# One layer of a streaming trunk: where the residual is added in the FFN down product

## The chip, the cores and the metric

The kernel runs on one core of a Trainium2 chip. The metric is the device time of one execution in microseconds (us). Before the change it is 1692.53 us, the median of three runs (1690.29 to 1696.99).

## The reference, cut to what matters

Everything is float32, 1024 tokens of width 1024. The change lies in the last product of the layer, the FFN down product, whose K is 3072 long, and in how its result is added to the residual stream `x`.

```python
D_MODEL, SEQ, D_FF = 1024, 1024, 3 * 1024
...
x = x + mix @ w_out[l]
h = rms_norm(x, norm2_w[l])
up = h @ ffn_w_up[l]
gate, val = jnp.split(up, [D_FF], axis=-1)
gate = causal_depthwise_conv(gate, ffn_conv_w[l], ffn_conv_b[l])
x = x + (jax.nn.gelu(gate) * val) @ ffn_w_down[l]
...
return rms_norm(x, norm_f_w)
```

## The kernel before, in words

All products run on TensorE (PE) in tiles of 128 x 512. To keep float32 precision, each operand is split into two parts (`split`, L167 and L168: ScalarE (ACT) casts the tile to a rounded part, VectorE (DVE) subtracts to get the rest), and three matmuls are done in place of one (`PASSES`).

Work is cut into jobs. A job has four results of 128 x 512, named (m, c), or (m, h) in a plain job. A plain job (`mm_std`, matmuls on L317) makes them with 96 matmuls. A fast job (`mm_fast`, matmuls on L347) uses seven products of 12 matmuls in place of eight (84 matmuls), on sums of blocks of both operands: on the weight side S1 to S4 (L235 to L251), on the other side T1 to T4 (`tsets`, L484 to L492). Its PSUM banks X, Y and Z are collected in two steps: `keep` copies a bank to SBUF on ACT (L362) while the bank goes on accumulating, and `total` adds a second bank on DVE (L371). Result (1, 0) alone comes out of bank X directly. A fast job is started before the one ahead of it has ended.

The FFN down product is the last stage. Its K of 3072 is cut into three groups g of 1024, and for each g there are four jobs t, of which t = 0 is plain and t = 1 to 3 are fast. Here the activations, written to DRAM (`ff_d`, L1006, by DMAs that GpSimd (POOL) issues) are the stationary blocks, loaded by L197 into `w` places, and the down weights `w_dn` are the moving operand, loaded by L1016 into `u` places and split there, or summed and split. The running sum over g is held in DRAM, in `x1_d`, which starts as the residual. For g < 2 each of the four results of a job is made so: a tile of `x1_d` is loaded (`pre_down`, L1052), DVE adds it (L365 in `keep` for three of the four results of a fast job, L1062 in `emit_down` for the other result and for all four of a plain job), and the sum is stored to `x1_d` (L1066). With g = 2 the sum stays in SBUF and goes into the final norm.

All loads and stores in this stage but those of L1006 are issued by SyncE (SP), which works through one list in order; an instruction that must wait holds up those behind it. The 78 `u` places are handed out oldest first, and a place that is handed out again is written only once its last user is done, which may be a DMA that still reads it. `build` makes the operand of the next group as long as at least 20 places are free. The order on each engine is set when the program is built, by a scheduler that goes by priority; `hp` raises it.

```python
def split(src, get=get):
    hi, lo = get(F32R), get(F32R)
    S.copy(hi, src)
    V.tensor_sub(lo, src, hi.bitcast(F32))
    return hi, lo
```

Of the kernel before, what the change touches and what calls it, by code (L numbers as in the profile page):

```python
# [15 lines left out]
ALU = mybir.AluOpType  # L16
# [68 lines left out]


class Units:
    """places of one shape in a pool, handed out oldest first in program order"""

    def __init__(self, pool, name, n, shape):  # L90
        self.pool, self.name, self.shape = pool, name, shape
# [7 lines left out]
    def get(self, dt=F32):  # L99
        i = self.q.popleft()  # L100
        self.count += 1
        t = self.pool.tile(self.shape, dt, tag=f"{self.name}{i}", name=f"{self.name}{i}_{self.count}")
        self.at[id(t)] = (i, t)
        return t

    def put(self, *tiles):
        for t in tiles:
            self.q.append(self.at.pop(id(t))[0])
# [20 lines left out]
def tile_trunk_layer(ctx, tc, x, positions, params, consts, normf, w_in, w_ro, w_lo,  # L129
                     w_out, w_up, w_dn, w_gate, out):  # L130
    nc = tc.nc
    V, S, G, PE, SY = nc.vector, nc.scalar, nc.gpsimd, nc.tensor, nc.sync
    ST = G if GQ else SY

    pool = ctx.enter_context(tc.tile_pool(name="sb", bufs=1))
# [8 lines left out]
    get, put = U.get, U.put  # L144
# [16 lines left out]
    def hp():  # L161
        return tc.high_priority(offset=1500)

    def split(src, get=get):
        """the two float32r parts of a float32 operand"""
        hi, lo = get(F32R), get(F32R)
        S.copy(hi, src)  # L167
        V.tensor_sub(lo, src, hi.bitcast(F32))  # L168
        return hi, lo
# [1 line left out]
    def drop(s):  # L171
        put(*s)

# [1 line left out]
    ORD_T = ("A11", "A12", "A21", "A22")  # L175

    class Job:
# [94 lines left out]
    back = deque()  # L272

    def build(budget, reserve=RESERVE):
        """go on with the operands that come next while there is room for them"""
        with hp():
            while builders and budget > 0 and len(U) >= reserve:
                c = next(builders[0], None)
                if c is None:
                    builders.popleft()  # L280
                else:
                    budget -= c
# [136 lines left out]
    def pair_src(w, i):  # L419
        return lambda m, kh: w[i, 2 * m + kh]  # L420

# [1 line left out]
    st = pool.tile([P, 16], F32, tag="st", name="st")  # L423
    nst = pool.tile([P, 5, 8], F32, tag="nst", name="nst")

    def rstd_of(dst, var, tmp):
        S.activation(tmp, var, AF.Sqrt)
        V.reciprocal(dst, tmp)
        V.tensor_mul(tmp, dst, dst)
        V.tensor_mul(tmp, tmp, var)  # L430
        V.tensor_scalar(tmp, tmp, -0.5, 1.5, ALU.mult, ALU.add)
        V.tensor_mul(dst, dst, tmp)

    def rms_scale(tiles, n, o=0):
        """1 / rms of n token tiles, one column each"""
        for t in range(n):
            for c in range(2):
                j = psa.get()
                if c == 0:
                    S.activation(j, tiles[t, c], AF.Square, accum_out=nst[:, c, o + t:o + t + 1])  # L440
                else:
                    V.scalar_tensor_tensor(j, tiles[t, c], 1.0, tiles[t, c], ALU.mult, ALU.mult,
                                           accum_out=nst[:, c, o + t:o + t + 1])
                psa.put(j)
        a, b, v, r, w = (nst[:, i, o:o + n] for i in range(5))
        V.tensor_add(v, a, b)
        V.tensor_scalar(v, v, 1.0 / D, EPS, ALU.mult, ALU.add)
        rstd_of(r, v, w)
        return r
# [56 lines left out]

    h1, keep = {}, {}

# [1 line left out]
    lt = pool.tile([P, 2, 8], F32, tag="lt", name="lt")  # L510
    lneg, lhalf = lt[:, 0, :], lt[:, 1, :]

# [17 lines left out]
        V.tensor_scalar(lhalf, s3, 4.0, None, ALU.mult)  # L530
        V.tensor_scalar(lneg, s3, -8.0, None, ALU.mult)

# [1 line left out]
    rot = {}  # L534

    def rotary_tables():
# [62 lines left out]
            rot["c", hf], rot["s", hf] = c, s  # L599
        put(pi_t, ang, m, a, f, r)  # L600

# [1 line left out]
    xl = {}  # L603
    tails = pool.tile([P, 2, 4], F32, tag="tails", name="tails")

# [96 lines left out]
        for w in wg:  # L702
            drop(w)

# [1 line left out]
    qk, vv, gg = {}, {}, {}  # L706
    rst = [pool.tile([P, 256], F32, tag=f"state{i}", name=f"state{i}") for i in range(2)]
    bst = pool.tile([P, 4, 6], F32, tag="bst", name="bst")
# [102 lines left out]
        if hd == HEADS - 1:  # L811
            put(*rot.values())

# [1 line left out]
    def emit_gate(which, n):  # L815
        def emit(m, h, src, unit):
            t = get() if unit is None else unit
# [3 lines left out]
        return emit  # L821

    def operand(op, fetch, sums=True):
        """the sets of an operand: first those of the plain product, then the sums"""
        for n in ("B11", "B21", "B12", "B22"):
            for j in range(4):
                t = fetch(n, j)
                op[n, j] = split(t)
                put(t)
                yield 0.6  # L830
        if sums:
            yield from tsets(op, fetch)
# [51 lines left out]
    gates = [(w, n) for n in range(4) for w in range(2)]  # L884
# [5 lines left out]
    for what in SEQ.split():  # L890
        if what == "g":
            add_gate()
        elif what[0] == "y":
            n = int(what[1])
            add(2 * n + 1, emit_y(n))
        elif what[0] == "x":
            n = int(what[1])
# [8 lines left out]
    def og_start(post=jobs[-2].post):  # L906
        builders.append(operand(og, from_dram(og_d), False))
        return post() if post else None
# [35 lines left out]
            mix[k, h] = split(mixf[k, h])  # L944
            put(mixf[k, h])

# [1 line left out]
    h2, keep2 = {}, {}  # L948
    for c in range(2):
        wo = {}  # L950
# [6 lines left out]
        for half in range(2):  # L957
            tl = {}
            for t in range(4):
# [4 lines left out]
                n = 0  # L964
# [22 lines left out]
            for w in wo.values():  # L987
                drop(w)

# [1 line left out]
    gv = {}  # L991

    def post_ff(i):
# [44 lines left out]
    run([Job(pair_src(w_up, i), h2, emit_to(gv), up_post(i), fast=i >= STD_U, last=i == NF - 1,  # L1038
             drop12=i == STD_U - 1) for i in range(NF)])

# [1 line left out]
    nf = []  # L1042
    fin = {}

    def x1_at(t, m, c):
        r0 = 512 * m + 128 * t
        return x1_d[r0:r0 + 128, TH * c:TH * c + TH]

    def pre_down(t):
        def pre(m, c):  # L1050
            acc = get()
            SY.dma_start(acc, x1_at(t, m, c))  # L1052
            return acc
        return pre

    def emit_down(g, t, fast):
        def emit(m, c, src, unit):
            if fast and unit is not None:
                acc = unit
            else:  # L1060
                acc = pre_down(t)(m, c)
                V.tensor_add(acc, src, acc)  # L1062
                if unit is not None:
                    put(unit)
            if g < 2:
                ST.dma_start(x1_at(t, m, c), acc)  # L1066
                put(acc)
                return
            fin[m, c] = acc
            square(m, c)  # L1070
            if (m, 1 - c) in fin:
                final(t, m)
        return emit

    def square(m, c):
        """what a finished tile adds to its rows' sum of squares; then the norm's weights"""
        j = psa.get()
        S.activation(j, fin[m, c], AF.Square, accum_out=nst[:, c, 2 + m:3 + m])
        psa.put(j)
        V.tensor_mul(fin[m, c], fin[m, c], nf[c])  # L1080
# [22 lines left out]
    def down_post(g, t):  # L1103
        def fn():
            if t == 2 and g < 2:
                builders.append(down_op(g + 1))
            if g == 1 and t == 3:
# [2 lines left out]

    run([Job(lambda m, kh, t=t, g=g: ff_d[g, 4 * m + t, kh].rearrange("p k c -> p (k c)"), dop[g],
             emit_down(g, t, t > 0), down_post(g, t), fast=t > 0, last=t == 3, drop12=t == 0,
             pre=(pre_down(t), ((0, 0), (0, 1), (1, 1))))
         for g in range(3) for t in range(4)])


def _pairs(w, cols):
    """[pair, 2 * (column half) + row half, partition, (row tile, column)]"""
    s = np.stack([w[:, np.asarray(c)] for c in cols]).reshape(len(cols), 2, 4, P, 2, P)
    return np.ascontiguousarray(s.transpose(0, 4, 1, 3, 2, 5)).reshape(len(cols), 4, P, 4 * P)  # L1120

# [47 lines left out]
```

## Time and profile before

One execution was profiled. Its span, from the first to the last instruction, is 1689.3 us, 3.2 us under the median of the three runs.

| | value |
|---|---|
| median of three runs | 1692.53 us |
| span of the profiled execution | 1689.3 us |
| PE busy over the span | 1634.8 us (97%) |
| DVE busy | 1253.0 us (74%) |
| ACT busy | 882.4 us (52%) |
| POOL busy | 40.7 us (2%) |
| DMA traffic | 221.78 MB, mean 131 GB/s |
| FFN down stage, matmuls | from 1414.93 us to the end |

PE is busy nearly all the time, so a change elsewhere counts where it makes PE idle or lets it go on. A matmul's row that carries an idle time in square brackets tells how long PE stood still before it, and what ended the wait. In the chain of work that ended last, the rows are in order of time: start, length, and the engine or DMA that held it.

### The profile page before, as it was taken

The page shows a single profiled execution, that of the slowest core. Times are in us where ns is not written, and L with a number is a line of the kernel's source. Part 1 is how long each engine was busy: PE and PEld are TensorE (multiplying, and loading weights), DVE is VectorE, ACT ScalarE, POOL GpSimd, SP SyncE. Part 2 cuts the span into 40 slices and gives each one's busy share as a digit, 9 for nine tenths or more (in the row PEclk, how much of TensorE's full clock was granted, in tenths as well). Part 3 has the DMA queues.
Part 4 walks back from the last instruction along what each step waited for, and adds up shares of the span by engine and source line. Part 5 has one row for each costly group of instructions (what it writes and reads, how often), then busy time and mean ns, then how long its engine had stood idle before and what let it go on. Part 6 is the DMA issues. An engine that isn't in the chain of part 4 may idle for free. (4 is left out here: it accounts for less than half of the span.)

```text
span 1689.3 us, 21180 instructions
## 1 busy us (share of the span) xinstructions
PE 1634.8 (97%) x7284; PEld 1341.8 (79%) x7284; DVE 1253.0 (74%) x2295; ACT 882.4 (52%) x1464; POOL 40.7 (2%) x60
## 2 busy tenths in 40 slices
PE   6999999999999999999999999999999999999997
PEld 5888888878887887878778788888888887777776
DVE  7986676675677878758871797677766778878786
ACT  6663434445578978743440465444444455444454
POOL 0010000000000000000000001000000000000000
PEclk9999999999999999999999999999999999999999
DMA  5243132231333427457553123222222236686852
GB/s 191 94 143 94 35 97 79 60 88 50 100 107 106 144 100 268 162 193 243 175 181 115 66 75 95 87 81 82 82 87 82 84 122 230 225 268 219 265 196 81
DMA packets 118220, 221.78 MB, mean 131 GB/s; under 512 B 13792, under 2 KB 13920, under 8 KB 118112
## 3 DMA queue, kind: packets, MB, share of 16 engines
q1 hardware_dynamic: 113888, 206.79, 37.3%
q0 software_dynamic: 4224, 13.64, 2.8%
q8 instruction: 57, 0.93, 0.2%
q14 instruction: 51, 0.42, 0.1%
HBM read 160.60 MB, written 54.53 MB: 127 GB/s over the span
## 5 line engine op out<-in xcount | busy, mean ns | idle before, releaser
L347 PE MATMUL g<-u,w 128*128 128x512 f32 x5124 | 1208.3, 394 | 23.8 <-ACT u L362 16.9
L347 PEld LDWEIGHTS g<-u,w 128*128 128x128 f32 x5124 | 962.0, 189 | 228.9 <-ACT u L362 22.7
L167 ACT CAST w<-w 128x512 fp32r<-128x512 f32 x471 | 290.7, 621 | 374.0 <-PE g L347 288.8
L168 DVE TENSOR_TENSOR w<-w,w 128x512 fp32r<-128x512 f32 x471 | 322.3, 686 | 97.0 <-ACT w L167 88.7
L317 PE MATMUL g<-u,w 128*128 128x512 f32 x1056 | 248.7, 392 | 0.0
L317 PEld LDWEIGHTS g<-u,w 128*128 128x128 f32 x1056 | 197.4, 188 | 41.7 <-ACT u L466 1.2
L167 ACT CAST u<-u 128x512 fp32r<-128x512 f32 x232 | 141.0, 620 | 164.1 <-DMA u<-w_dn 29.1
L168 DVE TENSOR_TENSOR u<-u,u 128x512 fp32r<-128x512 f32 x232 | 154.5, 686 | 31.8 <-ACT u L167 25.1
L371 DVE TENSOR_TENSOR u<-g,u 128x512 f32<-128x512 f32 x183 | 125.9, 688 | 69.1 <-PE g L347 48.8
L362 ACT COPY u<-g 128x512 f32<-128x512 f32 x183 | 106.4, 581 | 72.2 <-PE g L347 71.0
L968 PE MATMUL g<-u,u 128*128 128x512 f32 x384 | 89.6, 392 | 1.0 <-ACT u L167 1.0
L968 PEld LDWEIGHTS g<-u,u 128*128 128x128 f32 x384 | 71.6, 188 | 15.9 <-ACT u L167 1.4
L1001 DVE SCALAR_TENSOR_TENSOR u<-u,par,u 128x511 f32<-128x511 f32 (+1 forms) x96 | 71.7, 748 | 6.4 <-ACT u L998 5.6
L1006 POOL DMA_DIRECT2D ff_d<-u x48 | 36.1, 753 | 1296.0 <-DVE u L1005 1287.6
L235 DVE TENSOR_TENSOR w<-w,w 128x512 f32<-128x512 f32 x61 | 42.1, 690 | 21.5 <-DMA w<-w_up 9.2
L660 PE MATMUL a<-u,u 128*128 128x512 f32 x192 | 49.1, 401 | 3.9 <-ACT u L663 2.4
L998 ACT ACTIVATE u<-u,par 128x512 f32<-128x512 f32 x48 | 39.2, 816 | 18.6 <-DVE u L371 16.4
L660 PEld LDWEIGHTS a<-u,u 128*128 128x128 f32 x192 | 36.8, 194 | 12.9 <-ACT u L663 2.8
L970 DVE TENSOR_TENSOR u<-g,u 128x512 f32<-128x512 f32 x16 | 11.1, 691 | 47.2 <-PE g L968 47.2
L238 DVE TENSOR_TENSOR w<-w,w 128x512 f32<-128x512 f32 x61 | 42.0, 688 | 1.0
L244 DVE TENSOR_TENSOR w<-w,w 128x512 f32<-128x512 f32 x61 | 41.9, 687 | 0.6
L251 DVE TENSOR_TENSOR w<-w,w 128x512 f32<-128x512 f32 x61 | 41.9, 686 | 0.4
(160 smaller groups left out, 1073.2 us busy)
## 6 DMA issues: line engine op xcount, KB each, us to landing
w<-w_in SPq DMA_DIRECT2D x112, 256.0 KB, 2.6
w<-w_up SPq DMA_DIRECT2D x96, 256.0 KB, 2.6
u<-w_dn SPq DMA_DIRECT2D x96, 256.0 KB, 4.1
u<-x_d SPq DMA_DIRECT2D x56, 256.0 KB, 4.1
x_d<-u SPq DMA_DIRECT2D x48, 256.0 KB, 3.3
ff_d<-u POOLq DMA_DIRECT2D x48, 256.0 KB, 2.7
w<-ff_d SPq DMA_DIRECT2D x48, 256.0 KB, 3.8
u<-x SPq DMA_DIRECT2D x32, 256.0 KB, 5.2
```

The lines of the kernel that those rows point to most:

```text
L167: S.copy(hi, src)
L168: V.tensor_sub(lo, src, hi.bitcast(F32))
L235: V.tensor_add(s1, a21, a22)
L238: V.tensor_sub(s1, s1, a11)
L244: V.tensor_sub(a11, a11, a21)
L317: PE.matmul(ps[h], w[a][:, c], o[b], start=n == 0, stop=n == 23)
L347: PE.matmul(bank, w[a][:, c], need(op, (bn, j))[b], start=first and n == 0, stop=n == 11, skip_group_check=True)
L362: S.copy(u, bank)
L371: V.tensor_add(u, bank, u)
L660: PE.matmul(ps, wg[g][a][:, cs], xs[k][b], start=q == 0, stop=q == 5)
L968: PE.matmul(ps, o[a][:, 128 * t:128 * t + 128], wo[k][b], start=n == 0, stop=n == 23)
L1001: V.scalar_tensor_tensor(c[:, s:], src[:, :TH - s], w, c[:, s:], ALU.mult, ALU.add)
```

## The change

For g < 2 the tile of `x1_d` is no longer loaded, added on DVE and stored. The result tile in SBUF is sent by a DMA that adds to what stands in DRAM (`accum_op=ALU.add`), issued by POOL. Where a result lies in PSUM (all four of a plain job, one of a fast job), ACT copies it to SBUF first (L1063 of the new kernel), since a DMA is sent from SBUF; the other three are sent from where `total` left them. For g = 2 nothing changes. The remaining hunks of the diff take out docstrings and comments.

```diff
     def emit_down(g, t, fast):
         def emit(m, c, src, unit):
+            if g < 2:
+                acc = unit
+                if acc is None:
+                    acc = get()
+                    S.copy(acc, src)
+                G.dma_start(x1_at(t, m, c), acc, accum_op=ALU.add)
+                put(acc)
+                return
             if fast and unit is not None:
                 acc = unit
             else:
                 acc = pre_down(t)(m, c)
                 V.tensor_add(acc, src, acc)
                 if unit is not None:
                     put(unit)
-            if g < 2:
-                ST.dma_start(x1_at(t, m, c), acc)
-                put(acc)
-                return
             fin[m, c] = acc
...
     run([Job(lambda m, kh, t=t, g=g: ff_d[g, 4 * m + t, kh].rearrange("p k c -> p (k c)"), dop[g],
              emit_down(g, t, t > 0), down_post(g, t), fast=t > 0, last=t == 3, drop12=t == 0,
-             pre=(pre_down(t), ((0, 0), (0, 1), (1, 1))))
+             pre=(pre_down(t), ((0, 0), (0, 1), (1, 1)) if g == 2 else ()))
          for g in range(3) for t in range(4)])
```

Two places show how the order moves. The first is SP's list where the up product ends and the down product's first jobs begin; the names are place, count and tensor (`u54_1081` is place 54 of `u`). Before, loads of the residual stand there:

```order
L197 DMA w16_1112_12613<-ff_d_71 128x512
L1052 DMA u52_1075_12774<-x1_d_70 128x512
L197 DMA w3_1113_12615<-ff_d_71 128x512
L1052 DMA u61_1073_12734<-x1_d_70 128x512
L1052 DMA u25_1080_12868<-x1_d_70 128x512
L1016 DMA u20_1088_13063<-w_dn 128x512
L1052 DMA u72_1082_12927<-x1_d_70 128x512
```

With the change, on the same engine:

```order
L197 DMA w3_1113_12615<-ff_d_71 128x512
L1016 DMA u21_1090_13054<-w_dn 128x512
L1016 DMA u54_1081_13036<-w_dn 128x512
L1016 DMA u13_1093_13060<-w_dn 128x512
L1016 DMA u4_1084_13042<-w_dn 128x512
L197 DMA w17_1118_12682<-ff_d_71 128x512
L1016 DMA u33_1087_13048<-w_dn 128x512
L1016 DMA u54_1118_13146<-w_dn 128x512
```

The residual's loads are gone, and loads of the next group's weights have moved up into their room; place `u54` is loaded twice within seven rows. The casts that belong to these loads stand on ACT now like this, with the copy of the first fast job (`u16_1072`) behind them:

```order
L167 CAST u72_1082_13038<-u54_1081_13036 128x512
L1004 ACTIVATE u9_1038_12446<-u9_1038_12446 128x512
L167 CAST u35_1085_13044<-u4_1084_13042 128x512
L167 CAST u29_1068_12719<-u0_1055_12567 128x512
L167 CAST u20_1088_13050<-u33_1087_13048 128x512
L167 CAST u4_1119_13148<-u54_1118_13146 128x512
L362 COPY u16_1072_12728<-g4_215_12694 128x512
```

Four casts of the next group's weights (`u72`, `u35`, `u20` and `u4`) stand now ahead of that copy.

The second place is SP's list between the groups g = 0 and g = 1. Before, the stores and the loads of the residual stand between the loads of weights and activations, and a load of weights goes into a place that a store has just read (`u63`):

```order
L1066 DMA x1_d_70<-u63_1162_13288 128x512
L1066 DMA x1_d_70<-u45_1191_13432 128x512
L197 DMA w6_1187_13499<-ff_d_71 128x512
L1066 DMA x1_d_70<-u41_1192_13436 128x512
L1016 DMA u63_1183_13382<-w_dn 128x512
L197 DMA w0_1188_13501<-ff_d_71 128x512
```

With the change, on the same engine:

```order
L1016 DMA u68_1177_13354<-w_dn 128x512
L1016 DMA u77_1174_13348<-w_dn 128x512
L1016 DMA u77_1210_13835<-w_dn 128x512
L197 DMA w19_1182_13396<-ff_d_71 128x512
L1016 DMA u1_1201_13817<-w_dn 128x512
```

The weights' last load for that group stands now behind other loads of weights alone, and it goes into place `u77`, which an accumulating DMA has read. Those DMAs stand on POOL, here the ones of that boundary:

```order
L1064 DMA x1_d_70<-u66_1140_13208 128x512
L1064 DMA x1_d_70<-u77_1153_13255 128x512
L1064 DMA x1_d_70<-u76_1111_13114 128x512
L1064 DMA x1_d_70<-u45_1182_13398 128x512
L1064 DMA x1_d_70<-u19_1183_13401 128x512
```

POOL's list had nothing in this stage but the last four stores to `ff_d`; now 32 such rows follow or stand between them.

## The prediction

> **What bounds the kernel now.** I read the page's first lines, then PE's timeline of the last stage, then the chain, and last the windows and groups of that stage.
>
> ```profile
> span 1689.3 us, 21180 instructions
> PE 1634.8 (97%) x7284; PEld 1341.8 (79%) x7284; DVE 1253.0 (74%) x2295; ACT 882.4 (52%) x1464; POOL 40.7 (2%) x60
> ```
>
> PE is the bound, so the change can win only PE's idle time in the FFN down stage. These are the rows of PE in which it waited, between the first residual add and the last result of g = 1 and just behind; the bracket holds the wait:
>
> ```profile
> 1450.65 27.92 PE L347 MATMUL g<-u,w 128*128 128x512 f32 x120 [1.28 <-ACT u L167]
> 1480.26 22.12 PE L347 MATMUL g<-u,w 128*128 128x512 f32 x96 [1.68 <-ACT u L362]
> ...
> 1505.46 4.20 PE L347 MATMUL g<-u,w 128*128 128x512 f32 x12 [1.94 <-ACT u L362]
> ...
> 1540.01 0.51 PE L347 MATMUL g<-u,w 128*128 128x512 f32 x1 [1.46 <-ACT u L167]
> 1541.29 48.66 PE L347 MATMUL g<-u,w 128*128 128x512 f32 x206 [0.78 <-DVE u L168]
> ...
> 1592.70 3.04 PE L347 MATMUL g<-u,w 128*128 128x512 f32 x12 [1.62 <-ACT u L362]
> ...
> 1599.51 3.03 PE L347 MATMUL g<-u,w 128*128 128x512 f32 x12 [1.28 <-DVE u L371]
> ...
> 1637.45 37.20 PE L347 MATMUL g<-u,w 128*128 128x512 f32 x162 [1.81 <-ACT u L167]
> ```
>
> Together 1.28 + 1.68 + 1.94 + 1.46 + 0.78 + 1.62 + 1.28 + 1.81 = 11.85 us. All but the first two stand at the two passages from one group to the next. So **the whole stake is some 12 us, 0.7% of the kernel**, however much work on DVE and in DMAs goes away. About 0.5% (8.5 us) is what a measurement of this kernel can tell from no change.
>
> What PE waits for is the operand of the next group, which comes by DMA, ACT and DVE:
>
> ```profile
> 1495.00:1520.00 25.00, 23.03 (x93) 18.11 (x92) 20.50 (x34) 10.97 (x20) 0.00 (x0) 0.93 0.89 291
> ...
> 1595.00:1620.00 25.00, 23.72 (x105) 19.31 (x104) 24.37 (x41) 11.70 (x20) 0.00 (x0) 1.00 0.82 269
> ```
>
> The columns are the window, its length, busy time of PE, its weight loads, DVE, ACT and POOL, granted clock, DMA share and GB/s. At the first passage the 16 DMA engines are 89% busy; at the second DVE is busy 24.37 of 25 us. ACT has half its time free, POOL all.
>
> **What goes.** The groups of the stage give the adds, and the DMA list the transfers:
>
> ```profile
> L365 DVE TENSOR_TENSOR u<-u,u 128x512 f32<-128x512 f32 x27 | 18.4, 687 | 9.9 <-ACT u L362 6.9 <-DMA u<-x_d 3.0
> L362 ACT COPY u<-g 128x512 f32<-128x512 f32 x31 | 18.0, 581 | 17.3 <-PE g L347 17.3
> L1062 DVE TENSOR_TENSOR u<-g,u 128x512 f32<-128x512 f32 x21 | 14.0, 685 | 5.0 <-DMA u<-x_d 3.2 <-PE g L317 1.2 <-PE g L347 0.5
> ```
>
> Each serves three groups alike, so two thirds go: 18 adds of L365 and 14 of L1062, 32 x 0.69 = 22 us of DVE, in 190 us. Nearly all of it lies beside PE's matmuls and buys nothing by itself. With them go 32 loads and 32 stores from SP's list. I take the waits one by one.
>
> ```profile
> 1528.85 0.61 DVE u L1062
> 1529.48 3.09 DMA x_d<-u
> 1532.59 6.00 DMA u<-w_dn
> ...
> 1538.62 0.70 DVE u L484
> ```
>
> These rows of the chain are the passage from g = 0 to g = 1: the add of the last job's (1, 0), late in DVE's queue, its store, the load of weights into the place just stored, and the first DVE step of the last T set, which PE waited for (1.46 + 0.78 = **2.24 us**). With the change ACT copies that result. PE ends that bank with its row at 1505.46, at 1509.7, and ACT's list puts the copy among the first T sets, so I estimate 1515 us for it. The load then starts after the accumulating DMA's landing; taking 6 us for that (below) and 6.00 for the load gives about 1527 us, 11 us before PE wants it. This wait goes.
>
> ```profile
> 1618.74 0.61 DVE u L1062
> 1619.36 3.42 DMA x_d<-u
> 1622.81 3.94 DMA u<-x_d
> ```
>
> The second passage has the same shape: late add, store, a load into the same place, and DVE's queue behind it, up to PE's wait of **1.81 us** at 1637.45. It goes for the same reason; what is late next is the norm's work of g = 2, which stays.
>
> ```profile
> 1597.56 0.69 DVE L365 TENSOR_TENSOR u<-u,u 128x512 f32<-128x512 f32 x1 [0.40 <-DMA u<-x_d]
> 1598.17 0.68 DVE L484 TENSOR_TENSOR u<-u,u 128x512 f32<-128x512 f32 x1
> 1598.77 0.68 DVE L371 TENSOR_TENSOR u<-g,u 128x512 f32<-128x512 f32 x1
> ```
>
> Here the add of a residual tile, and its load, stood directly ahead of the L371 for which PE waited **1.28 us**. An add at DVE's pitch of 0.60 us, the wait of 0.40 and one more add in front go: I count the whole.
>
> ```profile
> 1478.59 0.62 ACT L167 CAST u<-u 128x512 fp32r<-128x512 f32 x1 [1.58 <-DMA x_d<-u]
> 1479.11 0.61 ACT L167 CAST w<-w 128x512 fp32r<-128x512 f32 x1
> 1479.63 0.58 ACT L362 COPY u<-g 128x512 f32<-128x512 f32 x1
> ```
>
> The three waits for L362 (1.68 + 1.94 + 1.62 = 5.24 us) are of another kind: ACT holds the copy that frees bank X behind a cast, here one whose place is still being stored; the chain ahead of the other two leads through loads of weights. SP issues those weights late in part because of the residual:
>
> ```profile
> SPq L1016 <- DMA x_d<-u: 10.2, 8, 2.6
> ```
>
> (us in total, times, longest). 10.2 us of SP's standing still with a load of weights behind a store go or turn into waits for an accumulating DMA, while the other waits, for PE and DVE to free places, stay. I count **half, 2.62 us**. The 1.28 us at 1450.65 belongs to the end of the up product; I count nothing. The gain is 2.24 + 1.81 + 1.28 + 2.62 = 7.95 us.
>
> **What comes.** 14 copies on ACT (L1063) at the 0.581 us of L362: 8.1 us in 190, on an engine that is busy 11 of 25 us; at nothing, hidden under ACT's free half, and at most 8.1 if each stood ahead of a copy of L362. POOL's 32 issues, at the 40.7 / 60 = 0.68 us of the page's first rows, stand on an engine with nothing else to do but four stores to `ff_d`, which g = 2 reads 100 us later; at nothing.
>
> ```profile
> u<-w_dn SPq DMA_DIRECT2D x89, 256.0 KB, 4.2
> u<-x_d SPq DMA_DIRECT2D x48, 256.0 KB, 4.1
> ...
> ff_d<-u POOLq DMA_DIRECT2D x4, 256.0 KB, 4.9
> ```
>
> The accumulating DMA itself stands nowhere in this trace. The rows are the stage's DMAs, with KB each and us to landing. Below, it is no quicker than a store from POOL of as many bytes, 4.9 us; above, it costs a load and then that store, 4.1 + 4.9 = 9.0 us. I take 6, nearer to the plain store, since one request is issued and not two. At 9.0 the passage above still has 8 us to spare; it costs PE something only from about 17 us on. In the DMA engines' time the ends are that of one store, 32 transfers fewer, and that of a load and a store, none fewer.
>
> Collectives: The Full Stack, section "The bandwidth ceiling: the fold count and why AG ≠ RS ≠ AR", in the Trainium skill, says that an add inside a DMA costs no time of its own but reads two sources through one ring, so that such transfers ran at about half the rate of copies. By that rule a DMA that adds 256 KB would occupy the engines like the load and the store that it replaces; the share of 0.89 would stay and the waits behind weights with it, and the sum below would be 2.6 us higher. No run here shows such a DMA yet.
>
> **What is queued anew.** Without the residual's loads, SP loads the next group's weights earlier, into few places: `u54` is loaded twice within seven rows, later a third time, and `u77` and `u1` likewise one group on. A second load waits for DVE's split of the first, then takes the 4.2 us of a load here, a cast of 0.62 and a subtraction of 0.69, 5.5 us; meanwhile DVE has about six rows of 0.60 before it. So 1.9 us of each stand open, and behind that cast on ACT stands the copy of L362, for which PE waits unless the product of 12 matmuls in between (3.0 us) covers it. There are six such loads. The ends are nothing and 6 x 5.5 = 33 us; by the nearest rows, 6 x 1.9 = 11.4 us before PE's cover. I take 0.5 us each, **3 us**.
>
> **Sum.** 1689.3 - 7.95 + 3 = 1684.3 us of span; the median of before lies 3.2 us above its span, so **1687.5 us**, 0.3% less than before.
>
> **The rivals.**
> *All waits go.* The reloads are covered, the operands of each group are ready early, and all 10.6 us of the waits behind 1450 go; and the matmuls after them run at the 37.20 / 162 = 0.230 us of the last long row in place of the 48.66 / 206 = 0.236, which is 1.2 us more there. That gives 1692.5 - 11.8, or 1681. For it: ACT's and POOL's free time. Against it: SP's and ACT's waits for places that PE frees, which don't go.
> *The DMA engines hold it.* The add takes as much of them as load and store together; weights land no earlier, and the 5.24 us stay, with the reloads' 3: 1692.5 - 5.3 + 3 = 1690. The share of 0.89 speaks for it, DVE's 24.37 of 25 us at the other passage, with a DMA share of 0.82, against.
> *Casts block the copy (the other side).* Each reload stands open by more than PE's cover, so that ACT's in-order list holds the copies of L362 of the first fast job in g = 0 and g = 1. At half of 33 us, the price is 16.5 and the time 1692.5 - 7.95 + 16.5 = 1701. It decides from 8.5 + 8 = 16.5 us over the six, 2.7 each. For it: the two loads of one place in the list. Against it: DVE's other rows between, and PE's product.
> *The adding DMA is slow.* Above 17 us to landing, SP stands behind it ten times or so in the two passages; at 25 us each passage loses 8, and the time is about 1701. Nothing in the trace comes near such a landing.
> That the change doesn't do what it says has little room: 32 such issues stand in POOL's list and the adds are gone from DVE's.
>
> **Chances.** The forecast's case 0.50, between 1683 and 1692; all waits go 0.20; the DMA engines hold it 0.12; casts block the copy 0.13; slow DMA 0.05. Faster by over 0.5% (under 1684.1) are the second case and 0.08 of the first: 0.28. Slower (over 1701) are the last two but for a part: 0.15, since the blocked copies' price is open upward. Within 0.5%: 0.57. The range for 8 in 10 goes from 1680, all waits gone, to 1701, the two slow cases at their prices.
>
> **What would show it.** In the new profile, PE's waits near 1540, 1599 and 1637 gone and those of L362 halved, the weights' last load of the passage issued near 1521, POOL's DMAs landing in 5 to 9 us. Wrong would be the forecast if PE waits for L362 in the first fast job of a group, behind a cast that waits for `w_dn` (the third rival), or if SP waits long for the accumulating DMAs (the fourth). A DMA share that stays at 0.89 with waits for weights as before is the second rival.

## The result, and the profile after

The changed kernel takes **1703.99 us** (median of 4 runs, 1700.88 to 1707.54) beside 1691.41 us for the kernel before on the same chip: ratio **1.0069, interval 1.0051 to 1.0088**, slower by 0.7% or 12 us. Forecast were 1687.5 us and a range up to 1701. The first lines of the page of after:

```profile
span 1705.4 us, 21130 instructions
PE 1637.3 (96%) x7284; PEld 1344.0 (79%) x7284; DVE 1234.2 (72%) x2263; ACT 889.2 (52%) x1478; POOL 68.4 (4%) x92
```

DVE lost 18.8 us of work, as meant, and PE does the same 7284 matmuls. The span is 16.1 us longer; 3.7 of that stand ahead of the stage (its first standard product starts at 1418.61 us in place of 1414.93), where both programs are alike. The stage itself grew from 274.4 to 286.8 us, by **12.4 us**, close to the 12.6 us between the medians. PE's timeline of the stage in after, the rows that began with a wait:

```profile
1456.38 24.77 PE L347 MATMUL g<-u,w 128*128 128x512 f32 x108 [0.21 <-ACT u L362]
1488.05 22.15 PE L347 MATMUL g<-u,w 128*128 128x512 f32 x84 [6.90 <-ACT u L362]
1513.14 4.29 PE L347 MATMUL g<-u,w 128*128 128x512 f32 x12 [2.94 <-ACT u L362]
1552.38 24.78 PE L347 MATMUL g<-u,w 128*128 128x512 f32 x108 [1.77 <-ACT u L362]
1580.10 22.24 PE L347 MATMUL g<-u,w 128*128 128x512 f32 x84 [2.94 <-ACT u L362]
1604.89 3.06 PE L347 MATMUL g<-u,w 128*128 128x512 f32 x12 [2.55 <-ACT u L362]
1610.60 5.76 PE L347 MATMUL g<-u,w 128*128 128x512 f32 x24 [1.52 <-ACT u L362]
1649.76 41.06 PE L347 MATMUL g<-u,w 128*128 128x512 f32 x179 [1.67 <-ACT u L167]
```

Against before, the waits near 1540 (for L167 and L168) and the one for L371 are gone. The waits for L362 grew from 5.24 to 0.21 + 6.90 + 2.94 + 1.77 + 2.94 + 2.55 + 1.52 = **18.83 us**, and with the 1.67 at the end PE waits 20.50 us where it waited 11.85: 8.65 more. The rest stands in the rows behind the waits: 84 matmuls take 22.15 and 22.24 us here and 19.38 us in a kernel without the wait (experiment 1). These two rows make 5.6 us, more than the 3.75 left to explain, since before too lost time in such rows: its 12 matmuls at 1505.46 took 4.20 us. The windows of after, in the columns of the prediction, show why:

```profile
1488.00:1494.00 6.00, 5.95 (x14) 4.68 (x15) 1.44 (x3) 0.94 (x2) 0.86 (x1) 0.50 0.45 90
1494.00:1510.00 16.00, 16.00 (x71) 13.05 (x70) 7.67 (x12) 5.70 (x11) 2.58 (x3) 1.00 0.83 216
...
1580.00:1586.00 6.00, 5.90 (x14) 4.66 (x15) 1.49 (x3) 0.94 (x3) 0.87 (x1) 0.50 0.46 87
```

For 6 us behind each of these two waits the granted clock is 0.50, and PE does 14 matmuls where the plain kernel of experiment 1 does 26 in the same place: some 2.8 us each time. What PE waits behind is seen in the waits of ACT and of SP's queue, and the DMA list (us in total, times, longest; below, KB each and us to landing):

```profile
ACT u L167 <- DMA u<-w_dn: 44.1, 22, 5.9
...
SPq L1016 <- DMA x_d<-u: 38.5, 7, 12.1
```

```profile
u<-w_dn SPq DMA_DIRECT2D x89, 256.0 KB, 4.9
...
x_d<-u POOLq DMA_DIRECT2D x32, 256.0 KB, 5.6
u<-x_d SPq DMA_DIRECT2D x16, 256.0 KB, 3.5
```

SP stood still for stores into x1 for 10.2 us before and stands still for adding DMAs for 38.5 us now. ACT's waits for weights grew from 26.4 to 44.1 us, and weights land in 4.9 us in place of 4.2. The adding DMA lands in 5.6 us. Not all of this comes from adding: with plain stores in the same lists (experiment 1) the three figures are 23.9, 31.0 and 4.7 us, so about half of what SP stands longer, and most of the weights' later landing, came with the rest of the change.

The longest wait step by step: rows of ACT, DVE, POOL and SP of after, between 1467 and 1488 us, with the wait ahead of each in brackets where there was one. PE waits here ahead of the twelfth of the group's 21 fast products (24 and 108 matmuls lie before it). In the program's order that is the fifth product of the second fast job.

```profile
1476.28 0.62 ACT L167 CAST u<-u 128x512 fp32r<-128x512 f32 x1 [2.73 <-issue]
...
1477.33 0.58 ACT L1063 COPY u<-g 128x512 f32<-128x512 f32 x1
...
1486.38 0.62 ACT L167 CAST u<-u 128x512 fp32r<-128x512 f32 x1 [5.59 <-DMA u<-w_dn]
1486.90 0.61 ACT L167 CAST w<-w 128x512 fp32r<-128x512 f32 x1
1487.42 0.58 ACT L362 COPY u<-g 128x512 f32<-128x512 f32 x1
```

```profile
1475.51 0.69 DVE L168 TENSOR_TENSOR u<-u,u 128x512 fp32r<-128x512 f32 x1 [1.56 <-issue]
```

```profile
1467.50 0.86 POOL L1064 DMA_DIRECT2D x_d<-u  x1 [1.54 <-DVE u L371]
1478.20 1.75 POOL L1064 DMA_DIRECT2D x_d<-u  x2 [9.84 <-ACT u L1063]
```

```profile
1482.55 0.33 SPq L1016 DMA_DIRECT2D u<-w_dn  x1
```

POOL issues the adding DMA of the first fast job's (1, 1) result at 1467.50; it lands in 7.9 us, at 1475.4. DVE's split at 1475.51 writes into that result's place (`u24` in the program's lists), and the cast at 1476.28 overwrites what the split reads. So both stand behind this DMA, though the profile calls their waits "issue"; at the same step of g = 1 it names the DMA, as DVE's wait of 2.10 us at 1567.59. Behind the cast, ACT copies the (1, 0) result of the first fast job at 1477.33. POOL issues its adding DMA at 1478.20. SP's next load of weights goes into that very place (`u36`), and is issued only at 1482.55, 4.35 us later, when the DMA has landed. It lands in 3.8 us; ACT's cast of it (1486.38) stands ahead of the copy of L362 (1487.42), which frees PE's bank: PE goes on at 1488.05. The same steps stand in front of the wait at 1580.10, in the second fast job of g = 1.

### The profile page after: what moved, and what is told of

It is laid out like the page before. It is cut to its first block, busy times and chain, and to the rows that moved or that the text cites. A ratio compares the mean times of both kernels' runs of the same rounds, so it can differ in the third digit from the quotient of the medians.

```text
span 1705.4 us, 21130 instructions
## 1 busy us (share of the span) xinstructions
PE 1637.3 (96%) x7284; PEld 1344.0 (79%) x7284; DVE 1234.2 (72%) x2263; ACT 889.2 (52%) x1478; POOL 68.4 (4%) x92
## 4 chain that ended last, share of the span: by engine, by line
PE 28%; issue 19%; DMA 4%; DVE 3%; POOL 2%; ACT 1%; SPq 0%; POOLq 0%; DVEq 0%; ACTq 0%
PE g L347 21%; PE g L968 4%; PE g L317 2%; DMA u<-u_d 1%; POOL x_d L1064 1%; POOL ff_d L1006 1%; DMA t_d<-u 1%; DVE u L168 1%; DMA x_d<-u 1%; DMA u_d<-u 1%; DMA u<-w_dn 1%; ACT u L167 0%; PE a L462 0%; DMA u<-w_out 0%; DMA w<-w_up 0%
## 5 line engine op out<-in xcount | busy, mean ns | idle before, releaser
L347 PE MATMUL g<-u,w 128*128 128x512 f32 x5124 | 1210.8, 395 | 34.7 <-ACT u L362 33.0
L347 PEld LDWEIGHTS g<-u,w 128*128 128x128 f32 x5124 | 964.4, 189 | 239.7 <-ACT u L362 39.7
L167 ACT CAST w<-w 128x512 fp32r<-128x512 f32 x471 | 290.5, 621 | 362.0 <-PE g L347 277.2
L168 DVE TENSOR_TENSOR w<-w,w 128x512 fp32r<-128x512 f32 x471 | 322.4, 686 | 102.3 <-ACT w L167 94.6
L167 ACT CAST u<-u 128x512 fp32r<-128x512 f32 x232 | 140.8, 620 | 180.4 <-DMA u<-w_dn 46.2
L168 DVE TENSOR_TENSOR u<-u,u 128x512 fp32r<-128x512 f32 x232 | 154.6, 687 | 49.3 <-ACT u L167 39.2
L371 DVE TENSOR_TENSOR u<-g,u 128x512 f32<-128x512 f32 x183 | 125.9, 688 | 80.7 <-PE g L347 49.4
L362 ACT COPY u<-g 128x512 f32<-128x512 f32 x183 | 106.4, 581 | 72.7 <-PE g L347 71.7
```

The costliest lines, as they stand in the source:

```text
L347: PE.matmul(bank, w[a][:, c], need(op, (bn, j))[b], start=first and n == 0, stop=n == 11, skip_group_check=True)
L362: S.copy(u, bank)
L371: V.tensor_add(u, bank, u)
```

## The experiments

Each kernel was timed in five rounds beside the kernel before on the same chip; 0.1% is 1.7 us. A ratio's interval is about 0.15% to either side, so the difference of two ratios is known to about 0.2%, some 4 us. Where a kernel stores plainly over the residual, the earlier sums are left out of its result. The theories: **DMA kind**, the adding DMA itself costs (later split into **engines**, the time that it takes of the 16 DMA engines, and **place**, the time for which it holds the result's place, so that weights and casts that go into it wait); **copy**, the copies of L1063 on ACT come too late; **order**, the new order of the lists costs, whatever the DMAs do.

**1. a1_plain_pool: the same lists, plain stores.**

```diff
-                G.dma_start(x1_at(t, m, c), acc, accum_op=ALU.add)
+                G.dma_start(x1_at(t, m, c), acc)
```

> The changed kernel with accum_op taken out of its 32 POOL issues: each result is stored plainly over the residual, so the earlier sums are left out. Every engine has the same list of instructions in the same order as in the changed kernel, which measured 1704 us. If the adding inside the DMA is the cost (theory 'DMA kind'), weights that go into a place just stored land sooner, the 6.9 us wait of PE for L362 goes, and the time falls to 1692 or below. If place reuse and the copies on ACT are the cost (theories 'place' and 'copy'), the same waits stand, each of PE's two long waits shorter by at most the 1 to 2 us that an adding DMA lands later than a plain one: 1699 to 1704 us.

Measured: 1685.95 us, ratio **0.9957 (0.9941 to 0.9973)**. With copies, places, reloads and order unchanged, taking the add out of 32 DMAs wins 1.0069 - 0.9957 = 1.12%, **19 us** (18 by the medians, as the expectations below say). This alone lets "copy" and "order" fall as causes by themselves. PE's row, and ACT's, POOL's and SP's, at the same place of the program as above:

```profile
1475.34 19.38 PE L347 MATMUL g<-u,w 128*128 128x512 f32 x84 [0.51 <-ACT u L362]
```

```profile
1466.31 0.62 ACT L167 CAST u<-u 128x512 fp32r<-128x512 f32 x1 [3.49 <-DVE u L168]
...
1467.36 0.58 ACT L1063 COPY u<-g 128x512 f32<-128x512 f32 x1
...
1473.66 0.62 ACT L167 CAST u<-u 128x512 fp32r<-128x512 f32 x1 [2.85 <-DMA u<-w_dn]
1474.19 0.61 ACT L167 CAST w<-w 128x512 fp32r<-128x512 f32 x1
1474.71 0.58 ACT L362 COPY u<-g 128x512 f32<-128x512 f32 x1
```

```profile
1461.18 0.54 POOL L1064 DMA_DIRECT2D x_d<-u  x1 [1.86 <-DVE u L371]
1468.23 0.54 POOL L1064 DMA_DIRECT2D x_d<-u  x1 [6.51 <-ACT u L1063]
```

```profile
1470.60 0.33 SPq L1016 DMA_DIRECT2D u<-w_dn  x1
```

From POOL's issue to SP's load pass 2.37 us in place of 4.35, from the load to PE's next matmul 4.74 in place of 5.50, and the copy itself comes 3.65 us earlier (from PE's row of 108 matmuls, 1456.38 and 1450.06, it is 20.95 and 17.30 us). The DMA of the (1, 1) result is issued 11.12 us behind that row in both kernels, but lands in 4.3 us here and in 7.9 there, so the split (at 1465.54), the cast and the copy behind it come earlier. The wait is 0.51 us in place of 6.90: 1.98 + 0.76 + 3.65 = 6.39 us less, nearly all of it time for which adding DMAs hold the places of two results longer. The profiled execution of after took 1707.54 us, its longest, and that of a1_plain_pool 1678.30, its shortest, so their rows differ by more than the medians do. The DMA lists of this stretch tell why places are held longer and loads are late, after (1455 to 1490) first, then the plain kernel (1449 to 1480):

```profile
q0 software_dynamic: 986, 1.95, 35.2%
...
x_d<-u POOLq DMA_DIRECT2D x7, 256.0 KB, 4.3
...
u<-w_dn SPq DMA_DIRECT2D x3, 256.0 KB, 6.0
```

```profile
q0 software_dynamic: 704, 2.29, 20.0%
...
x_d<-u POOLq DMA_DIRECT2D x7, 256.0 KB, 2.4
...
u<-w_dn SPq DMA_DIRECT2D x4, 256.0 KB, 3.2
```

(Queue: packets, MB, share of 16 engines.) Seven adding DMAs land in 4.3 us, seven plain ones in 2.4; and the weights beside them, which add nothing, land in 6.0 and in 3.2.

**What an adding DMA takes of the engines.** The queues' shares over 290 us of after (1400 to 1690), 270 us of a1_plain_pool (1400 to 1670) and 280 us of before (1400 to 1680), in this order:

```profile
q0 software_dynamic: 4928, 9.44, 19.5%
```

```profile
q0 software_dynamic: 2880, 9.44, 9.2%
```

```profile
q1 hardware_dynamic: 32550, 59.26, 64.0%
q0 software_dynamic: 320, 1.05, 1.1%
```

Four stores to `ff_d` are in each q0; before, they took 1.1% of 280 = 3.1 us. An adding DMA so takes (0.195 x 290 - 3.1) / 32 = **1.67 us** of all 16 engines, a plain store (0.092 x 270 - 3.1) / 32 = 0.68, and a load or store of before 0.640 x 280 / 226 = 0.79 (226 times 256 KB in 59.26 MB). So an adding DMA takes as much as the load and the store that it replaces, 1.59. Collectives: The Full Stack, section "The bandwidth ceiling: the fold count and why AG ≠ RS ≠ AR", in the Trainium skill has the adding transfers of ring collectives at half the rate of copies. The 1.67 against 0.68 us of this case agrees with its direction and is 2.5 times.

**2. Places of their own, with adding (a2_own_places) and without (a8_own_plain).** Six of the 78 places serve the results of g = 0 and g = 1 alone, so no weights go into a place that an adding DMA reads; 14 places in place of 20 are kept free. The two kernels have the same lists.

```diff
-                    acc = get()
+                    acc = E.get()
...
-                put(acc)
+                E.put(acc)
```

> The changed kernel with six of the 78 operand places set aside for the results of g = 0 and g = 1, so that no load of weights goes into a place that an adding DMA still reads; the sum is complete. Theory 'place': SP's longest wait for an adding DMA (12.1 us) falls under 4 us, PE's waits for L362 fall from about 19 us to 8 or less, and the time is 1686 to 1693 us. Theory 'copy' (ACT issues the copies late, and the casts that wait for weights hold L362): waits shrink only in part, 1695 to 1701 us. Theory 'order' (fewer free places, other order): nothing gained, above 1701 us.

> The kernel with six places of its own (1692.8 us) with plain stores in place of adding DMAs, in the same order on every engine; earlier sums are left out, as in a1_plain_pool. With places of their own no weights wait for the results' DMAs. If the adding DMA costs only through the places that it holds longer (theory 'place'), nothing is left for it to cost: 1690 to 1694 us, and the 7 us above a1_plain_pool are the order's. If it costs through the time that it takes of the 16 DMA engines, so that other transfers land later (theory 'engines'), the plain one is faster here too: 1684 to 1687 us.

Measured: adding 1692.81 us, **1.0004 (0.9994 to 1.0013)**; plain 1683.48 us, **0.9948 (0.9928 to 0.9967)**. The first wins 11 us on the change, as "place" had it; none of SP's waits is for a store or an adding DMA into x1 any more. But without any such wait adding still costs 0.56%, 9.5 us: the "engines" theory's answer. Where they lie is seen in the stretch of 20 us ahead of PE's wait in the third fast job of g = 0, in the lists and then in PE's next row, adding (1490 to 1510) and plain (1488 to 1508):

```profile
q0 software_dynamic: 439, 0.79, 29.7%
...
u<-w_dn SPq DMA_DIRECT2D x12, 256.0 KB, 6.3
```

```profile
q0 software_dynamic: 240, 0.79, 10.1%
...
u<-w_dn SPq DMA_DIRECT2D x14, 256.0 KB, 4.3
```

```profile
1509.02 5.49 PE L351 MATMUL g<-u,w 128*128 128x512 f32 x12 [4.26 <-ACT u L366]
```

```profile
1505.12 4.60 PE L351 MATMUL g<-u,w 128*128 128x512 f32 x12 [2.44 <-ACT u L366]
```

(L351 and L366 are L347 and L362 there.) Three adding DMAs take 30% of the engines for 20 us, and twelve loads of weights land in 6.3 us instead of 4.3.

**3. Double the suspected cost: each plain store twice, in places of their own (a12_own_twice) and in the changed kernel's order (a15_twice).**

```diff
                 G.dma_start(x1_at(t, m, c), acc)
+                r0 = 512 * m + 128 * t
+                G.dma_start(p_d[g, r0:r0 + 128, TH * c:TH * c + TH], acc)
```

> a8_own_plain (1683.5 us: plain stores, six places of their own, earlier sums left out) with each plain store issued twice, the second time into a scratch tensor; the order of PE, DVE, ACT and SP is unchanged, nothing is added anywhere. A plain store took 0.68 us of all 16 DMA engines, so twice is 1.36 us beside the 1.7 us of an adding DMA. If the adding DMA costs through the engines' time (theory 'engines'), some two thirds of the 9.3 us between a8_own_plain and a2_own_places come: 1688 to 1692 us. If the cost is something that only adding has, 1683 to 1686 us.

> a1_plain_pool (plain stores in the changed kernel's order, 0.9957 of before; earlier sums left out) with each store issued twice, the second time into a scratch tensor; PE, DVE and SP keep their order, nothing is added. If engines' time and hold make the loss of 18 us and adding has nothing of its own, the doubled store, with 1.36 us of the engines beside 1.7 for an adding one, gives about two thirds of it: 1695 to 1700 us. If adding itself makes the loss (reading what it adds to, say), the hold alone is left: 1688 to 1691 us.

Measured: 1688.50 us, 0.9981 (0.9969 to 0.9992), and 1696.00 us, 1.0013 (1.0001 to 1.0025). With places of their own the second store costs 0.33%, 5.6 us, within what "engines" expected: it adds the time of one store, 0.7 us, where adding adds about 1.1 (1.8 less 0.7, from the shares of these kernels), and 5.6 of 9.5 us come, near the share of the engines' time (0.7 of 1.1). So these runs need no cost that only adding has there, and can't exclude a small one. In the changed kernel's order it costs 0.56%, 9.5 us, half of the 19; 1696.00 us is at the lower end of the 1695 to 1700 that engines' time and hold together were expected to give.

**4. Hold the place longer without more bytes (a13_hold).**

```diff
                 G.dma_start(x1_at(t, m, c), acc)
+                G.dma_start(x1_at(t, m, c)[0:1, :], acc[0:1, :])
```

> a1_plain_pool (1686 us: plain stores, earlier sums left out, the changed kernel's order on PE) with a second store behind each, of one row of 2 KB out of the same place to the same row, so that the place is free only when this one too has landed: held longer by a landing (some 2 to 4 us), with hardly any bytes more. Theory 'place': half of the 18 us between all plain and all adding is the hold, so 1692 to 1697 us. If the engines' time alone counts: 1684 to 1688 us.

Measured: 1690.01 us, 0.9981 (0.9964 to 0.9997): 0.24%, 4 us above a1_plain_pool, between the two expectations. The second store is issued when the first has landed (3.5 us) and lands 2.7 us later, so the place is held at least as long as by an adding DMA. But the 4 us are no larger than what two ratios can tell apart, and two things beside the hold have changed: POOL waits 71.2 us in its list for first stores to land, which delays later results, and the lists of DVE, ACT and SP differ in some rows from those of a1_plain_pool. In its trace PE waits 2.93 us at 1451.77 and then does 204 matmuls without a wait, across the place of the 6.90. So the price of the hold alone is between nothing and some 8 us, not shown more closely. With places of their own, in another order, adding costs 9.5 us less than in the changed kernel's (19 less 9.5, experiment 2).

**5. Which of the 32 results (a9_add14, a10_add01): parts of the adding in the changed kernel's order.**

```diff
+                kw = dict(accum_op=ALU.add) if t < 2 else {}
-                G.dma_start(x1_at(t, m, c), acc, accum_op=ALU.add)
+                G.dma_start(x1_at(t, m, c), acc, **kw)
```

(a10_add01; a9_add14 adds where ACT copied the result.)

> The changed kernel in its own order, with adding DMAs for the 14 results that ACT copies out of PSUM (L1063) and plain stores for the 18 that DVE leaves in SBUF (L371); of those 18 the earlier sums are left out. All plain gave 1686 us, all adding 1704. If the cost is the engines' time, it goes with the number: 1686 + 14/32 x 18 = 1694 us. If it hangs on the copies that ACT issues late ((1,0) of the fast jobs, whose place is loaded with weights at once), nearly all of it stays: 1699 to 1704. If it hangs on the 18 results of DVE, 1686 to 1690.

> The changed kernel in its own order, with adding DMAs for the results of the standard job and the first fast job of g = 0 and g = 1 (16 of the 32), and plain stores for those of the second and third fast jobs, whose earlier sums are left out. Theory 'place': the places that the operand of the next group and the first fast job's T sets are built into come back in these two jobs, where PE's waits of 6.9 and 2.9 us stand; 1697 to 1702 us. Theory 'engines': half of the adding DMAs, half of the cost, 1695 us, and lower if the transfers at the passages, where the DMA engines are 85 to 93% busy, carry it: 1688 to 1692.

Measured: a9 1688.57 us, 0.9977 (0.9963 to 0.9991); a10 1694.40 us, 1.0017 (1.0005 to 1.0029). The 14 copied results cost 0.20%, 3.4 us, so most hangs on the 18 that DVE leaves in SBUF. The (1, 0) results are among the 14, so their hold is the smaller part of the loss. PE's row in a9 at the place of the longest wait:

```profile
1481.39 20.95 PE L347 MATMUL g<-u,w 128*128 128x512 f32 x84 [3.75 <-ACT u L362]
```

From POOL's issue of the (1, 0) result (1472.69) to SP's load (1476.99) pass 4.30 us, as in after, and PE waits 3.75 us, between the 0.51 of a1_plain_pool and the 6.90 of after; at the same place of g = 1 it waits 0.29.

Half of the adding, in the first two jobs, costs 0.60%, 10 us of 19: as much as goes by number, as "engines" expected.

**6. The parts of the change alone: the 14 copied results (a7_copy14; a14_copy14_plain is the same order with plain stores) and the 18 others (a6_fast18).** What isn't added by DMA goes by load, DVE and SP's store as before.

```diff
-                acc = unit
-                if acc is None:
+                if unit is not None:
+                    acc = unit
+                    ST.dma_start(x1_at(t, m, c), acc)
+                else:
                     acc = get()
                     S.copy(acc, src)
                     G.dma_start(x1_at(t, m, c), acc, accum_op=ALU.add)
```

> Adding DMAs for the 14 results in PSUM alone (copied by ACT); the other 18 as in the kernel before: load, add by DVE before the total, store by SP. The sum is complete. In a9_add14 adding for these 14 cost 2.6 us over all plain. The loads and stores of the 18 come back, and the DMA engines' time is about that of before; the late add of (1, 0) and its store behind it are gone. Theory 'engines': near before, 1687 to 1694 us. Theory 'place': an adding DMA still stands ahead of weights in the place of (1, 0), 1696 us or more.

> a7_copy14 (1706.7 us) with plain stores for the 14 copied results, in the same order on every engine; their earlier sums are left out. If adding for these 14 is what makes it slow (in the place of (1, 0) that weights go into), it falls to 1690 to 1696 us. If that order itself is slow, 1700 us or more.

> The other part alone: adding DMAs for the 18 results that DVE leaves in SBUF, the 14 in PSUM as in the kernel before. The sum is complete. By a9_add14 these 18 carried 15 of the 18 us of the adding: 1693 to 1702 us. If the parts don't cost apart what they cost together (the copies on ACT being needed for the loss), 1688 to 1693.

Measured: 1706.70 us, 1.0085 (1.0070 to 1.0101); with plain stores 1696.04 us, 1.0021 (1.0010 to 1.0032); the 18 alone 1697.74 us, 1.0032 (1.0018 to 1.0045). The 14 adding DMAs cost 0.64%, 11 us, in this order and 3.4 in the other. So the price of one is not a constant. That it depends on what is loaded beside it and on what goes into its place is likely, but not shown. Which of the 14 it is here was not traced further.

**7. Copies on DVE (a3_dve_copy), places given back four results later (c_late4_16), and a control (b5_lim24).** The edits: `V.tensor_copy(acc, src)` for `S.copy(acc, src)`; a queue of four places ahead of `put(acc)`, with 16 places kept free; the kernel before with 24 places kept free in the stage in place of 20.

> The changed kernel with the 14 copies of L1063 on DVE in place of ACT; the adding DMAs stay, and the places. Theory 'copy': the copy no longer stands behind ACT's casts that wait for w_dn, POOL issues earlier, and the two PE waits for L362 at about 1488 and 1580 us (6.9 and 2.9 us) go: 1690 to 1696 us. Theory 'place': the load still stands behind an adding DMA that was issued just before, 1700 to 1705 us.

> The changed kernel with one edit and its counterweight: a result's place is given back four results later than before, so that its adding DMA has landed by the time that the place is used again, and operands are built ahead down to 16 free places in place of 20, since four are held. The sum is complete. Theory 'place': SP's longest wait for an adding DMA falls under 5 us and the time to 1686 to 1694 us. Theory 'engines': 1698 us or more.

> A control: the kernel before, with the number of free places from which operands are built ahead raised to 24 in the down stage alone. Nothing of the residual is changed, only the order and the places. If the stage's time hangs on the order as such (theory 'order'), it moves by 5 us or more to either side of 1691; if not, it stays within 4 us of it.

Measured: 1715.48 us, 1.0132 (1.0115 to 1.0148); 1699.56 us, 1.0036 (1.0020 to 1.0051); 1695.58 us, 1.0016 (1.0003 to 1.0028). Moving the copies to DVE makes it worse than either theory expected, so "copy" has no support; but DVE has 14 copies more to do there, and the clean test of "copy" is experiment 1. The late return won 0.33% of the change's loss, but SP still waited up to 9.5 us for an adding DMA: four results don't make a fixed time, and fewer places were free for building ahead, so it doesn't decide between "place" and "engines", though its time lies where "engines" expected it. The control moved by 2.7 us: this change of the order is worth some tenths of a per cent. One control doesn't bound what another order costs; that the order doesn't make the 19 us is shown by experiment 1, where it is the same.

**8. A version that keeps the gain (v1_three, v2_slow2, v3_own_slow2).** Plain stores of g = 0 and g = 1 into two tensors, which g = 2 loads and adds.

```diff
-                G.dma_start(x1_at(t, m, c), acc, accum_op=ALU.add)
+                G.dma_start(part_at(g, t, m, c), acc)
...
+            SY.dma_start(acc, x1_at(t, m, c))
+            SY.dma_start(b, part_at(0, t, m, c))
+            SY.dma_start(d, part_at(1, t, m, c))
+            V.tensor_add(acc, acc, b)
+            V.tensor_add(acc, acc, d)
```

> A version meant to beat both: the results of g = 0 and g = 1 are stored plainly into two tensors of their own, and for g = 2 the residual and the two parts are loaded and added by DVE a job ahead (32 loads and 32 adds more there, where a1_plain_pool shows a DMA share of 0.32 and 0.22 and no operand is built). The sum is complete. Theory 'engines': the passages run as in a1_plain_pool (1686 us) and the adds lie in free time: 1684 to 1690 us. It fails if g = 2 is held by DVE, 24.98 of 30 us busy there in a1_plain_pool: 32 x 0.69 = 22 us more would then cost up to 10 us, 1696.

> v1_three (1708.0 us) with the sums for g = 2 made at most two results ahead, spread over the jobs, instead of a whole job ahead. The sum is complete. If v1_three lost its 22 us over a1_plain_pool to the 12 loads and 8 adds in the second passage, most of it comes back: 1686 to 1696 us. If DVE's or SP's work in g = 2 as such holds PE, it stays above 1700.

> The same with the six places of their own for the results of g = 0 and g = 1 (a8_own_plain, 1683.5 us). The sum is complete. 1684 to 1695 us, some 2 us under v2_slow2, if the second passage is not held by the sums.

Measured: 1708.03 us, 1.0095 (1.0077 to 1.0113), above all that was expected; 1690.01 us, 0.9987 (0.9974 to 1.0001); 1690.03 us, **0.9983 (0.9970 to 0.9996)**. The window of v1_three at the second passage:

```profile
1620.00:1650.00 30.00, 19.12 (x68) 13.58 (x67) 28.43 (x61) 12.54 (x26) 0.00 (x0) 0.78 0.85 286
```

PE is busy 19.12 of 30 us there, DVE 28.43. In v3_own_slow2 DVE is as busy in the same window (28.27 us) and PE has 26.08, so DVE's load alone isn't the reason. The chain of v1_three leads through loads of the parts there (4.69 us from 1640.78): that a job's sums made at once fall on the passage is likely, not shown. Spread over the jobs they cost little; places of their own, expected to win 2 us more, won nothing. The last version is 0.9% faster than the changed kernel and 0.2% faster than before, less than the 0.5% at which a difference counts here.

## Why the prediction was wrong

- **The work that goes and the copies** were priced rightly as a whole. a1_plain_pool is the change in all but the add, reloads and copies included, and takes 0.43% (7.3 us, 4.6 to 10 by its interval) off; the working without a price for the DMA had 7.95 - 3 = 4.95 us off. That agreement is partly luck: of the 2.62 us counted for L362 only 0.69 came (5.24 to 4.55, below), while the 1.28 at 1450.65, counted at nothing, went. ACT's 14 copies cost nothing to be seen; POOL's issues took 0.86 us, not 0.68, and nothing waited for that.
- **The passages.** Of the 5.33 us counted, 2.24 near 1540 and 1.28 at L371 went; the 1.81 at the second passage stayed (1.67 at 1649.76; 0.76 with plain stores). L362 gave new waits near two of those that went: 1.77 at 1552.38, a few matmuls behind where those of 1540 stood, and 1.52 near where that of L371 was.
- **The failed step is the adding DMA's own price, and with it "half" of L362's 5.24 us.** Its landing, forecast at 6 us, was 5.6, and up to 7.9. Wrong was "it costs PE something only from about 17 us on". That slack was read at the passage, for one load that has 11 us to spare. The results of the first fast job have none: the places of its (1, 1) and (1, 0) results are written again at once, by a split and by a load of weights. The first DMA, landing later, holds up that split, a cast and the copy of (1, 0) behind it; the second then holds up the load, the cast of that load and behind it the copy of L362, until PE waits in the second fast job (6.90 at 1488.05), with the half clock on top. Even with plain stores L362's waits don't halve: 0.19 + 0.51 + 1.20 + 0.86 + 0.71 + 1.08 = 4.55 us in a1_plain_pool.
- **The bounds of the DMA engines' time stood in the text ("a load and a store, none fewer"), but no term of the sum took them.** 1.67 us a transfer is that upper end. The rival built on it, "the DMA engines hold it" (1690, chance 0.12), had the mechanism and much too small a price: it kept the old waits, where the new load of the engines falls on the loads of weights that ACT's casts wait for. A likely reason, not shown by a run: in SP's list the residual's loads could come early and spread out; an adding DMA falls when the result is there.
- **"Casts block the copy" (1701, 0.13) came near in time, but by luck.** PE does wait for L362 behind a cast that waits for `w_dn`. But in the first fast job, which it named, that is 0.21 and 1.77 us; the 6.90 and the 2.94 at 1580.10 stand in the second. And its cause was wrong: the reloads are all there in a1_plain_pool, where the waits for L362 are 4.55 us.
- **"The adding DMA is slow" (1701, 0.05)** had its sign, SP's long waits for adding DMAs (38.5 us, 12.1 the longest), but not its cause: the landing is 5.6 us, not above 17, and SP stands for 23.9 us behind plain stores too.
- How the 19 us split stays partly open: the hold cost 4 us in a13_hold, which is not clear of noise, and adding without any hold of SP's loads 9.5 (own places, another order). In the longest wait nearly all of the 6.39 us is places held longer, but they are held longer because the DMAs land later. Hold and engines' time act on the same casts, and no run shows them apart in the changed kernel's own order.

## What to carry to other kernels

An adding DMA spares the engine's add and the requests, not the DMA engines' time: count it as the load and the store that it replaces, and look at what else is in flight when the result comes. A slack found at one place of a loop isn't the slack of the next: for every place that comes back, ask what is written into it first, and which in-order list stands behind that. Whether a change moves cost or removes it is shown fastest by the same lists with the suspected operation made plain, and that operation's cost by doubling it.

## What was not expected of the hardware

- The adding DMA of 256 KB took 1.67 us of the 16 engines against 0.68 for a plain store from the same queue, and its issue 0.86 us of POOL against 0.54. Loads beside it landed in 6.0 to 6.3 us against 3.2 to 4.3.
- In after, waits on PE of 6.90 and 2.94 us (at 1488.05 and 1580.10) were followed by 6 us at a granted clock of 0.50; behind 2.55 us (at 1604.89) 12 matmuls took 3.06 us, the full rate. TensorE: Matmul & The Clock Gate, section "What's actually happening", in the Trainium skill gives about 3.4 us of idling for the fall to half clock; here less was enough. In before even 1.94 us (at 1505.46) was followed by 0.50, from 1507 to 1510. So in these traces the length of the last wait alone doesn't tell whether the clock falls.
